# Six token tiles of an encoder block turned on VectorE in 32 by 32 blocks and by way of DRAM instead of on TensorE, with a fixed order of the second product's tiles and one convolution sum moved ahead

## The chip, the cores and the metric

The kernel runs on one core of one Trainium2 chip. The core has five engines that run their own instruction streams and wait for each other by semaphores: TensorE (PE in the profile; PEld is its weight load), VectorE (DVE), ScalarE (ACT), GpSimd (POOL) and SyncE (SP), which here issues nearly all transfers (DMAs). The metric is the device time of one launch in microseconds. Three runs of the kernel before took 1248.94, 1249.9 and 1251.17 us; their median is 1249.9 us.

## The reference

One layer of a hybrid encoder over two groups of tokens, 1024 "prompt" tokens and 256 "sample" tokens, 1024 features each, all in float32:

```python
def trunk(x, ...):
    h = rms_norm(x, norms[i, 0])
    mix = short_conv_mixer(h, conv_w_in, conv_w, conv_w_out)
    x = x + rms_norm(mix, norms[i, 1])
    h = rms_norm(x, norms[i, 2])
    return x + rms_norm(swiglu(h, ffn_w_in, ffn_w_out), norms[i, 3])

def short_conv_mixer(x, w_in, conv_w, w_out):
    b, c, v = jnp.split(x @ w_in, 3, axis=-1)      # w_in: 1024 x 3072
    u = c * v                                       # conv of width 3 over the tokens
    conv = sum(up[:, j:j + S] * conv_w[j] for j in range(3))
    return (b * conv) @ w_out                       # w_out: 1024 x 1024

def swiglu(x, w_in, w_out):                         # w_in: 1024 x 5632, w_out: 2816 x 1024
    gate, up = jnp.split(x @ w_in, 2, axis=-1)
    return (jax.nn.silu(gate) * up) @ w_out
```

With one layer (DEPTH = 1) the mLSTM mixer of the reference is never reached.

## The kernel before

Every product is done as three matmuls on float32 values split into a high and a low part (`split`: ScalarE rounds the high part, VectorE subtracts it; `TERMS` lists the three pairs). The large products are also done in Strassen-Winograd fashion, 7 products of half blocks in place of 8, so sums of blocks (`sums`, S1 to S4) are made for weights and activations by VectorE.

The kernel has four stages. **First product** (w1 and the convolution): channels lie on the partitions. Its first blocks are written out by hand in `start`; the others go through `Block` and are put in order by a scheduler that uses its own estimates. The results b * conv are stored to DRAM (`zd`) in split form. **Second product** (w2): here tokens lie on the partitions. There are ten tiles of 128 tokens, in the order ORDER2 = 0, 4, 1, 5, 2, 6, 3, 7, 8, 9; tiles 8 and 9 are the sample tokens. For each tile `load_z` brings its 1 MB of `zd` into `zs`, `mm2` does 48 matmuls of 128x512 into two PSUM banks `mx`, and then follow `norm_squares` (ScalarE, squares of `mx` summed into `j_n`), `norm_factor` (VectorE and GpSimd on single columns, `n_3t` and the like, numbered by tile), `norm_residual` (two reads of `mx` by VectorE, then the addition of `x`, whose result `x1` is stored to DRAM by SyncE), `norm_squares2` (ScalarE), `norm_factor2` and `norm_end` (VectorE; its result is `ht`). **Third product** (w3, gate and up) needs `ht` with features on the partitions, so `transposes` turns each `ht`: eight 128x128 transposes on TensorE into two PSUM banks (`tr`), which ScalarE and VectorE copy into the block buffers `ar` (a11, a12, a21, a22). `early_sums` makes parts and sums of these blocks for 128 columns at a time, and `make` prepares the first weight unit F0 (`wrf`) as `g`, `u`, `sums`, `t24`, `t13`. `entry` is the passage between the two products, written out by hand: products of tiles 8 and 9, the turning of the last tiles, the remaining sums, and the first blocks of the third product (`xf`, `yf`, `zf`). **Fourth product** (w4) follows, its order planned by the kernel's own table of costs.

In `start` the first two blocks of the w1 product are interleaved by hand; one of their additions is `ev3.add22`, which adds the bank `zb` to a copy (`c__749` in the profile); the bank is written again by a later product.

The tiles of the second product stand in a loop outside any hand-written order, so the scheduler orders them; inside `with tc.manual_schedule()` (`start`, `entry`) the instructions stand on each engine as the program text has them. Memory is handed out in places: 23 of kind "b", three of kind "a", two of kind "s"; a place that is freed goes to the end of its list, and whoever takes it waits for the last use of it. PSUM has eight banks, taken in turn. SyncE issues its transfers in order; one that waits holds up those behind it.

Of the kernel before, what the change touches and what calls it, by code (L numbers as in the profile page):

```python
# [8 lines left out]
F32 = mybir.dt.float32  # L9
F32R = mybir.dt.float32r  # L10
# [4 lines left out]
P = 128  # L15
# [21 lines left out]
def encoder_kernel(ctx: ExitStack, tc: tile.TileContext, xT, x, g0T, gB, cwT, w1, w2, w3, w4, out_p, out_s):  # L37
# [45 lines left out]


    zd = dram.tile([2, len(UNITS), P, 2, KD, P], F32, tag="zd", name="zd")
    x1d = dram.tile([NT, P, D], F32, tag="x1d", name="x1d")
    actd = dram.tile([len(UNITS), KP, P, 14 * P], F32, tag="actd", name="actd")

# [97 lines left out]
    def make(u, what):  # L186

        if u is None:
            return
        rw = raw[u]  # L190
        if what == "sums":
            sub(rw[:, 0], rw[:, 1], rw[:, 0])
            sub(rw[:, 1], rw[:, 2], rw[:, 1])
            sub(rw[:, 2], rw[:, 0], rw[:, 2])
            add(rw[:, 3], rw[:, 3], rw[:, 2])
            return
        blocks = {"g": slice(0, 4, 3), "u": slice(1, 3), "t13": slice(0, 2), "t24": slice(2, 4)}[what]
        t = wb[what, u] = get(f"w{what}{uname(u)}_", [2, 2, 512], F32R)
        split(t[:, 0], t[:, 1], rw[:, blocks])
        sums_made[u] = sums_made.get(u, 0) + what.startswith("t")  # L200
        if sums_made[u] == 2:
            put(raw.pop(u))
# [353 lines left out]
    def start():  # L556
# [209 lines left out]
        ev3.times(0, 0, ev3.t["11"])  # L766
        ev3.copy22(b3.bank["x"])
        ev.end()
        make(un, "u")
        b3.sample(evac=False)  # L770
        b3.run("x", "t24", 1, "a22", False)
# [1 line left out]
        ev3.samp_of(0, b3.bank["sg"])  # L773
        ev3.read21(b3.bank["x"])
        make(un, "sums")
        ev3.add22(b3.bank["z"])
        make(un, "t24")
        b3.run("z", "u", 1, "s4", False)
        b3.release_u()
# [26 lines left out]
    def load_z(i, k0=0, k1=KD):  # L806
        if i not in zs:
            zs[i] = get(f"zs{i}", [2, KD, P], F32R)
        src = zd[i // 4, i % 4] if i < 8 else zd[i - 8, 4]
        nc.sync.dma_start(f32(zs[i][:, :, k0:k1]), src[:, :, k0:k1])  # L810
# [35 lines left out]
    def transposes(i, banks=(None, None)):  # L846
# [17 lines left out]
                left.append((i, q, ov))  # L864
        put(hts.pop(i))

    left = []

    def take_left():
# [6 lines left out]
    def mm2(*tiles, ks=range(KD)):  # L876
        for i in tiles:
            if i not in mx:
                mx[i] = [new_ps(f"mx{i}_{h}", MX_BANKS.get((i, h))) for h in range(2)]
        for k in ks:  # L880
            for i in tiles:
                for j, (w, part) in enumerate(TERMS):
                    for h in range(2):
                        nc.tensor.matmul(  # L884
                            mx[i][h], zs[i][:, part, k], w2t[k][:, w, h * H : (h + 1) * H],
                            start=k == 0 and j == 0, stop=k == KD - 1 and j == 2,
                        )
# [35 lines left out]
        )  # L923
        put(x1)

    def after_mm2(i):
        for step in (norm_squares, norm_factor, norm_residual, norm_squares2, norm_factor2, norm_end):
            step(i)

    xts = {}  # L930

    def load_xt(i):
        xts[i] = get(f"xt{i}", [D], kind="a")
        nc.sync.dma_start(xts[i], x[i])


    a11, a12, a21, a22 = ar[0, 0], ar[1, 0], ar[0, 1], ar[1, 1]

    def early_sums(t):

        a, b, d = (q[:, :, t] for q in (a11, a21, a22))
        split(*(q[:, :, t] for q in cb["a11"]), a)
        add(b, b, d)
        sub(a, a, b)
        add(s3[:, :, t], d, a)

    F0, F1, F2 = (("f", f) for f in range(3))
    for i in ORDER2[:2]:
        load_z(i, KD - 2, KD)
    for i in ORDER2[:2]:  # L950
        load_xt(i)
    for n, i in enumerate(ORDER2[:8]):
        if n == 0:
            mm2(i, ORDER2[1])
        elif n > 1:
            early = KD - 2 if n < 4 else 4
            mm2(i, ks=range(early))
            transposes(ORDER2[n - 2])
            mm2(i, ks=range(early, KD))
            if n == 4:  # L960
                cb["a11"] = [get(f"a11{p}", [KH, 512], F32R) for p in "hl"]
                s3 = get("s3", [KH, 512])
                early_sums(slice(0, P))
            if n == 6:
                early_sums(slice(P, 2 * P))
        after_mm2(i)
        if n:
            load_z(ORDER2[n + 1])
            load_xt(ORDER2[n + 1])
        if n == 4:  # L970
            load(F0)
            for what in ("g", "u", "sums"):
                make(F0, what)
        if n == 6:
            for what in ("t24", "t13"):
                make(F0, what)


    A11, S1, S2, S4, A12, S3, A22 = range(7)
# [120 lines left out]
    def entry():  # L1100

        load_z(9)
        load(F1)
        early_sums(slice(2 * P, 3 * P))
        mm2(8, ks=range(1))
        transposes(ORDER2[6], (6, 7))
        mm2(8, ks=range(1, KD))
        norm_squares(8)
        load_xt(9)
        mm2(9, ks=range(1))  # L1110
        put(w2t[0])
        transposes(ORDER2[7], (0, 1))
        norm_factor(8)
        for k in range(1, KD):
            mm2(9, ks=range(k, k + 1))
            put(w2t[k])
        early_sums(slice(3 * P, 4 * P))
        high, low = parts_of("a12", a12)
        both(high)
        both(low)  # L1120
        make(F1, "g")
        high, low = parts_of("s2", a11)
        both(high)
        both(low)
        e0, e1 = EvF(0), EvF(1)
        b0 = Block(F0, e0, banks={q: new_ps(f"{q}f0_", b) for q, b in (("x", 6), ("y", 7))})
        b1 = Block(F1, e1, F2, ("f", 3), banks={q: new_ps(f"{q}f1_", b) for q, b in (("x", 0), ("y", 1))})
        b0.run("x", "g", 0, "a11", True)
        b0.run("y", "g", 1, "a12", True)
        b1.run("x", "g", 0, "a11", True)  # L1130
        b1.run("y", "g", 1, "a12", True)
        high, low = parts_of("s1", a21)
        both(high)
        norm_squares(9)
        norm_residual(8)
        e0.read11(b0.bank["x"])
        both(low)
        put(a21)
        norm_squares2(8)
        norm_factor(9)  # L1140
        add(e0.c11, e0.c11, b0.bank["y"])
        high, low = parts_of("s3", s3)
        both(high)
        norm_factor2(8)
        norm_residual(9)
        norm_end(8)
        e1.read11(b1.bank["x"])
        norm_squares2(9)
        add(e1.c11, e1.c11, b1.bank["y"])
        both(low)  # L1150
        put(s3)
        high, low = parts_of("a22", a22)
        both(high)
        norm_factor2(9)
        e0.silu11()
        b0.run("x", "t24", 0, "s2", False)
        e0.read12(b0.bank["x"])
        e1.silu11()
        b0.bank["z"] = new_ps("zf0_", 4)
        b0.run("z", "t13", 0, "s1", True)  # L1160
        both(low)
        put(a22)
        hs[:] = [get(f"hs{b}", [KH, 2, 256], F32R) for b in (0, 1)]
        transposes(8, (5, 2))
        b0.run("x", "t13", 1, "s3", False)
        b0.drop("t13")
        add(a12, a12, a11)
        put(a11)
        norm_end(9)
        put(gb)  # L1170
        high, low = parts_of("s4", a12)
        e0.copy22(b0.bank["x"])
        both(high)
        take_left()
        both(low)
        put(a12)
        transposes(9, (3, 1))
        b0.run("x", "t24", 1, "a22", False)
        b0.drop("t24")
        take_left()  # L1180
        add(e0.c22, e0.c22, b0.bank["z"])
        e0.read21(b0.bank["x"])
        b0.run("z", "u", 1, "s4", False)
        make(F1, "u")
        make(F1, "sums")
        e0.add12(b0.bank["z"])
        make(F1, "t24")
        b0.bank.update(sg=new_ps("sgf0_", 7), su=new_ps("suf0_", 2))
        b0.half = True
        b0.sample()  # L1190
        make(F1, "t13")
        b1.bank.update({q: new_ps(f"{q}f1_", b) for q, b in (("z", 6), ("sg", 3), ("su", 5))})
        turn[0] = 7
        load(F2)
        return b1

    def ffn_in(f):
        units = [("f", g) if g < KF else None for g in (f, f + 1, f + 2)]
        if f == 0:
            with tc.manual_schedule():  # L1200
                second.append(entry())
        elif f == 1:
            b = second[0]
            for what in ("g", "u", "sums"):
                make(F2, what)
            b.p657()
            b.sample()
            b.p43()
        else:
            b = Block(units[0], EvF(f), *units[1:], final=f == KF - 1)  # L1210
            b.p12()
            b.p657()
            b.sample()
            b.p43()
        if f % 2 and f < KF - 1:
            for _ in spill(f // 2):
                pass
# [450 lines left out]
```

## Time and profile before

| what | value |
|---|---|
| median of three timed runs | 1249.9 us |
| the profiled execution's own time | 1248.29 us |
| its span (first to last instruction) | 1246.5 us |
| granted TensorE clock | 0.998 |
| second product, first matmul of `mx` to first matmul of `xf` | 313.0 to 430.2 us |

The profile's page lists busy time by engine, the chain of work that ended last, and groups of instructions. Its further answers give waits (who waited for whom), a timeline (start, duration, engine, line, operation with its tiles, and in brackets the idle time before it and what ended it), and, for a stretch of time, the transfers with the share of the 16 DMA engines' time that their packets took. Names of tiles stand as out<-in; SPq marks the issue of a transfer by SyncE.

### The profile page before, as it was taken

To read this page: it belongs to the slowest core of one execution; us is meant where nothing else is said; L and a number is where in the kernel's file an instruction comes from. 1 tells how busy PE (TensorE), PEld (TensorE's weight loads), DVE (VectorE), ACT (ScalarE), POOL (GpSimd) and SP (SyncE) were. 2 spreads that over 40 slices of the span, in tenths; PEclk is the share of its full clock that TensorE was granted. 3 is DMA by queue.
4 is the path that set the end of the run, shared out by engine and by line. 5 is a ranking of instruction groups with operands and counts; after the bars stand their busy time and mean duration, and the time that the engine had idled before them with its cause. 6 is when DMAs were issued, how large, how long until landed. Compare 5 with 4: busy or idle time off the path is not lost.

```text
span 1246.5 us, 14942 instructions
## 1 busy us (share of the span) xinstructions
PE 1231.8 (99%) x5695; PEld 1022.9 (82%) x5695; DVE 863.1 (69%) x1225; ACT 485.5 (39%) x755; POOL 25.6 (2%) x49
## 2 busy tenths in 40 slices
PE   9999999999999999999999999999999999999997
PEld 6887888888888888888888888888888888888886
DVE  6986866758376688576576675765768478869566
ACT  8643433325233554343344343444435342202011
POOL 0000000000011000000000000000000000000000
PEclk9999999999999999999999999999999999999999
DMA  8323141416844215254352452542526798856894
GB/s 306 122 81 114 38 130 57 118 51 215 308 175 165 100 51 167 86 178 127 110 186 94 151 160 89 182 129 88 194 96 208 255 316 304 281 202 222 288 324 182
DMA packets 186120, 207.31 MB, mean 166 GB/s; under 512 B 8000, under 2 KB 146368, under 8 KB 185024
## 3 DMA queue, kind: packets, MB, share of 16 engines
q1 hardware_dynamic: 185616, 205.83, 49.1%
q8 instruction: 45, 0.74, 0.2%
q10 hardware_dynamic: 432, 0.53, 0.1%
q14 instruction: 27, 0.22, 0.1%
HBM read 134.89 MB, written 71.43 MB: 166 GB/s over the span
## 4 chain that ended last, share of the span: by engine, by line
PE 95%; DVE 1%; DMA 1%; ACT 1%; issue 1%; POOL 0%; SPq 0%; POOLq 0%; DVEq 0%
PE xo L1467 12%; PE mx L884 8%; PE zo L1467 6%; PE yo L1467 3%; PE xp__1018 L213 1%; PE xp__1382 L213 1%; PE xf__3815 L213 1%; PE xf__3359 L213 1%; PE xf__7249 L213 1%; PE xf__7082 L213 1%; PE xf__6881 L213 1%; PE xf__6719 L213 1%; PE xf__6518 L213 1%; PE xf__6356 L213 1%; PE xf__6155 L213 1%; PE xf__5993 L213 1%
## 5 line engine op out<-in xcount | busy, mean ns | idle before, releaser
L884 PE MATMUL mx<-w2s,zs 128*128 128x512 f32 x480 | 111.1, 391 | 0.0
L884 PEld LDWEIGHTS mx<-w2s,zs 128*128 128x128 f32 x480 | 89.5, 188 | 18.2
L106 ACT ACTIVATE st<-act 128x640 fp32r<-128x640 f32 x77 | 56.8, 737 | 92.2 <-DMA actd<-st 55.3
L97 DVE TENSOR_TENSOR st<-act,st 128x640 fp32r<-128x640 f32 x77 | 63.2, 821 | 20.3 <-ACT st L106 19.8
L100 DVE TENSOR_TENSOR y<-y,xo 128x512 f32<-128x512 f32 x85 | 58.2, 685 | 27.4 <-PE xo L1467 27.1
L1467 PE MATMUL xo<-w4t,us 128*128 128x512 f32 x273 | 68.9, 389 | 0.0
L1467 PEld LDWEIGHTS xo<-w4t,us 128*128 128x128 f32 x273 | 51.3, 188 | 10.6
L1467 PE MATMUL xo<-w4t,ut 128*128 128x512 f32 x222 | 55.5, 389 | 0.0
L106 ACT ACTIVATE w4t<-w4r 128x1024 fp32r<-128x1024 f32 (+1 forms) x23 | 23.5, 1023 | 72.4 <-DVE w4r L97 59.4
L1467 PEld LDWEIGHTS xo<-w4t,ut 128*128 128x128 f32 x222 | 41.7, 188 | 8.7
L100 DVE TENSOR_TENSOR y<-y,zo 128x512 f32<-128x512 f32 x45 | 30.8, 685 | 17.3 <-PE zo L1467 17.0
L1467 PE MATMUL xo<-w4b,ut 128*128 128x512 f32 x165 | 41.6, 390 | 0.0
L1467 PE MATMUL zo<-w4t,ut 128*128 128x512 f32 x165 | 41.5, 389 | 0.0
L1467 PE MATMUL zo<-w4b,ut 128*128 128x512 f32 x165 | 41.5, 389 | 0.0
L1499 ACT ACTIVATE junk<-y 128x1024 f32<-128x1024 f32 (+1 forms) x12 | 11.0, 919 | 73.7 <-DVE y L100 72.4
L1467 PEld LDWEIGHTS xo<-w4b,ut 128*128 128x128 f32 x165 | 31.0, 188 | 6.6
L1467 PEld LDWEIGHTS zo<-w4t,ut 128*128 128x128 f32 x165 | 31.0, 188 | 6.5
L1467 PEld LDWEIGHTS zo<-w4b,ut 128*128 128x128 f32 x165 | 31.0, 188 | 6.4
L459 DVE SCALAR_TENSOR_TENSOR row<-u,cw,row 128x1024 f32<-128x1024 f32 (+1 forms) x32 | 27.7, 880 | 3.3 <-ACT row L457 3.0
L106 ACT ACTIVATE w4b<-w4r 128x512 fp32r<-128x512 f32 (+1 forms) x22 | 18.1, 840 | 28.2 <-DMA us<-actd 16.0
L1467 PE MATMUL yo<-w4b,us 128*128 128x512 f32 x114 | 28.9, 389 | 0.0
L97 DVE TENSOR_TENSOR w4t<-w4r,w4t 128x1024 fp32r<-128x1024 f32 (+1 forms) x23 | 26.9, 1173 | 0.8 <-ACT w4t L106 0.8
(2372 smaller groups left out, 3313.9 us busy)
## 6 DMA issues: line engine op xcount, KB each, us to landing
actd<-st SPq DMA_DIRECT2D x154, 320.0 KB, 2.6
ut<-actd SPq DMA_DIRECT2D x20, 1024.0 KB, 7.1
us<-actd SPq DMA_DIRECT2D x62, 256.0 KB, 4.8
ut<-actd SPq DMA_DIRECT2D x16, 768.0 KB, 8.1
zd<-zst SPq DMA_DIRECT2D x32, 320.0 KB, 3.3
zs<-zd SPq DMA_DIRECT2D x8, 1024.0 KB, 6.6
w4r<-w SPq DMA_DIRECT2D x11, 512.0 KB, 4.1
w4r<-w SPq DMA_DIRECT2D x22, 256.0 KB, 5.6
```

What stands on the lines that cost most here:

```text
L97: nc.vector.tensor_tensor(out=out, in0=a, in1=b, op=ALU.subtract)
L100: return nc.vector.tensor_tensor(out=out, in0=a, in1=b, op=ALU.add)
L106: nc.scalar.activation(out, a, AF.Copy)
L213: nc.tensor.matmul(out[:, :n], stat(w, k), mov(part, k), start=first and k == 0 and j == 0, stop=last and k == KH - 1 and j == 2, skip_gro ...
L459: nc.vector.scalar_tensor_tensor(out=out, in0=src, scalar=cw[:, j, dd : dd + 1], in1=out, op0=ALU.mult, op1=ALU.add)
L884: nc.tensor.matmul(mx[i][h], zs[i][:, part, k], w2t[k][:, w, h * H : (h + 1) * H], start=k == 0 and j == 0, stop=k == KD - 1 and j == 2,)
L1467: nc.tensor.matmul(acc, stat[n, c, j][:, ap], w[wp], start=starts and jn == 0 and m == 0, stop=jn == len(grp) - 1 and m == 2, skip_group_c ...
L1499: nc.scalar.activation(junk, src, AF.Square, accum_out=acc[:, col : col + 1])
```

## The change

Tiles 0 to 5 of the second product's order (the first six) are no longer turned on TensorE. VectorE turns each `ht` in blocks of 32 by 32 (`turn_blocks`, result `vt`, in a place of kind "a"); four DMAs write `vt` to a new DRAM buffer `hd` in pieces of 32 numbers (`turn_out`); two DMAs bring it back as blocks of `ar` (`turn_in`). The seventh and the eighth tile (3 and 7) are still turned by TensorE, in `entry`. The loop over the first eight tiles becomes a function `tiles`, which now stands within the hand-written order, so all its steps follow one another on every engine as written. Two weight loads that stood early (F0) move into the fourth step, the `zs` loads run two tiles ahead, and the third part of `early_sums` moves from `entry` to the eighth step. In `start`, `ev3.add22` moves before the weight parts of the next unit.

```diff
+    hd = dram.tile([6, P, KD, P], F32, tag="hd", name="hd")
...
         ev.end()
+        ev3.add22(b3.bank["z"])
         make(un, "u")
...
         make(un, "sums")
-        ev3.add22(b3.bank["z"])
         make(un, "t24")
...
+    def turn_blocks(i):
+        h = hts.pop(i)
+        v = turned[i] = get(f"vt{i}", [4, KD, 32], kind="a")
+        nc.vector.transpose(v.rearrange("p q k t -> p k q t"), h.rearrange("p (k j q) -> p k q j", j=32, q=4))
+        put(h)
+
+    def turn_out(n):
+        v = turned.pop(ORDER2[n])
+        dst = hd[n].rearrange("(j q) k t -> j (q k) t", q=4)
+        for g in range(4):
+            nc.sync.dma_start(
+                dst[:, :, 32 * g : 32 * g + 32], v[32 * g : 32 * g + 32].rearrange("j q k t -> j (q k) t")
+            )
+        put(v)
+
+    def turn_in(n):
+        i = ORDER2[n]
+        for q in range(2):
+            nc.sync.dma_start(ar[q, i // 4][:, :, i % 4 * P : i % 4 * P + P], hd[n, :, 4 * q : 4 * q + 4])
...
-    for n, i in enumerate(ORDER2[:8]):
-        if n == 0:
-            mm2(i, ORDER2[1])
-        elif n > 1:
-            early = KD - 2 if n < 4 else 4
-            mm2(i, ks=range(early))
-            transposes(ORDER2[n - 2])
-            mm2(i, ks=range(early, KD))
...
+    def tiles():
...
+        load_z(ORDER2[2])
+        mm2(*ORDER2[:2])
+        for n, i in enumerate(ORDER2[:8]):
+            if n > 1:
+                mm2(i)
+            norm_squares(i)
+            if n != 1 and max(3, n + 2) < 9:
+                load_z(ORDER2[max(3, n + 2)])
+            if 0 < n <= VIA:
+                turn_out(n - 1)
+            norm_factor(i)
+            norm_residual(i)
+            if n:
+                load_xt(ORDER2[n + 1])
+            norm_squares2(i)
+            if 0 < n <= VIA:
+                turn_in(n - 1)
+            if n == 3:
+                load(F0)
             if n == 4:
...
+                new_parts("a11")
                 early_sums(slice(0, P))
+            if n == 5:
+                make(F0, "g")
+                make(F0, "u")
             if n == 6:
                 early_sums(slice(P, 2 * P))
...
+            if n == 7:
+                early_sums(slice(2 * P, 3 * P))
+            norm_factor2(i)
+            if n == 7:
+                make(F0, "t24")
+            norm_end(i)
+            if n < VIA:
+                turn_blocks(i)
+            if n == 6:
+                make(F0, "sums")
+            if n == 7:
+                make(F0, "t13")
...
             with tc.manual_schedule():
+                tiles()
                 second.append(entry())
```

Three places where the order on an engine moves are shown. The first is VectorE at tile 3, the seventh of the order. Before, the block copy of tile 3's neighbour and its sums stand behind `ht`:

```order
L141 SCALAR_TENSOR_TENSOR n_3t<-n_3_3061,rq 128x1
L122 TENSOR_SCALAR n_3t<-n_3t 128x1
L905 SCALAR_TENSOR_TENSOR x_3_3071<-mx_0_2994,n_3t,gb 128x512
L905 SCALAR_TENSOR_TENSOR x_3_3071<-mx_1_2995,n_3t,gb 128x512
L100 TENSOR_TENSOR x_3_3071<-x_3_3071,xt_2992 128x1024
L100 TENSOR_TENSOR n_3t<-n_3_3076 128x1
L122 TENSOR_SCALAR n_3t<-n_3t 128x1
L921 SCALAR_TENSOR_TENSOR ht_3085<-x_3_3071,n_3t,gb 128x1024
L858 COPY ar_2442<-tr_1_3129 128x4x128
```

Of the change, the same tile: the part `a11l` and the three sums (`ar`, `ar`, `s`) stand ahead of the second factor and of `ht`, and F0's weight sums (`wrf`) between `ht` and the next tile's first factor.

```order
L929 SCALAR_TENSOR_TENSOR x_3_3055<-mx_1_2990,n_3t,gb 128x512
L101 TENSOR_TENSOR x_3_3055<-x_3_3055,xt_2966 128x1024
L95 TENSOR_TENSOR a11l<-ar_2440,a11h 128x4x128
L101 TENSOR_TENSOR ar_2441<-ar_2441,ar_2443 128x4x128
L98 TENSOR_TENSOR ar_2440<-ar_2440,ar_2441 128x4x128
L101 TENSOR_TENSOR s_2881<-ar_2443,ar_2440 128x4x128
L101 TENSOR_TENSOR n_3t<-n_3_3062 128x1
L123 TENSOR_SCALAR n_3t<-n_3t 128x1
L945 SCALAR_TENSOR_TENSOR ht_3078<-x_3_3055,n_3t,gb 128x1024
L98 TENSOR_TENSOR wrf__2788<-wrf__2788 128x512 x3
L101 TENSOR_TENSOR wrf__2788<-wrf__2788 128x512
L142 SCALAR_TENSOR_TENSOR n_7t<-n_7_3134,rq 128x1
```

The second place is SyncE at the load of tile 9 (`zs_3185` before, `zs_3173` in the change). Before, it stands ahead of the store of tile 3's `x1`:

```order
L910 DMA x1d<-x_6_2974 128x1024
L934 DMA xt_3089<-x 128x1024
L810 DMA zs_3185<-zd 128x2048
L910 DMA x1d<-x_3_3071 128x1024
L934 DMA xt_3187<-x 128x1024
```

Of the change, it stands behind the store of tile 7's `x1`, two tiles later, and the stores of the turned blocks (`hd<-vt`) and their loads (`ar<-hd`) stand among the others:

```order
L881 DMA hd<-vt_2987 1024x1x32 x4
L934 DMA x1d<-x_3_3055 128x1024
L954 DMA xt_3060<-x 128x1024
L889 DMA ar_2441<-hd 128x4x128
L889 DMA ar_2443<-hd 128x4x128
L934 DMA x1d<-x_7_3144 128x1024
L954 DMA xt_3149<-x 128x1024
L811 DMA zs_3173<-zd 128x2048
```

The third place is VectorE in `start`. Before, the addition of the bank `zb` (`c__749`) stands behind the weight sums (`wrp__581`) of the next unit:

```order
L94 TENSOR_TENSOR wup__757<-wrp__581,wup__757 128x1024
L100 TENSOR_TENSOR sp__804<-sp__804,sgb__713 128x256
L103 TENSOR_TENSOR row_155<-row_155,sp__804 128x2x128
L103 TENSOR_TENSOR row_155<-row_155,xb__621 128x512
L94 TENSOR_TENSOR zst_809<-row_155,zst_809 128x640
...
L100 TENSOR_TENSOR wrp__581<-wrp__581 128x512
L100 TENSOR_TENSOR c__749<-c__749,zb__712 128x512
L94 TENSOR_TENSOR wt24p__824<-wrp__581,wt24p__824 128x1024
```

Of the change, it stands ahead of all of these:

```order
L101 TENSOR_TENSOR c__750<-c__750,zb__713 128x512
L95 TENSOR_TENSOR wup__759<-wrp__582,wup__759 128x1024
L101 TENSOR_TENSOR sp__806<-sp__806,sgb__714 128x256
L104 TENSOR_TENSOR row_156<-row_156,sp__806 128x2x128
L104 TENSOR_TENSOR row_156<-row_156,xb__622 128x512
L95 TENSOR_TENSOR zst_811<-row_156,zst_811 128x640
```

More of the change, by code (lines that the diff above doesn't have):

```diff
@@ L865, in transposes @@
         put(hts.pop(i))
+    turned = {}
+    def turn_blocks(i):
[15 more added lines that the diff above has]
+            nc.sync.dma_start(ar[q, i // 4][:, :, i % 4 * P : i % 4 * P + P], hd[n, :, 4 * q : 4 * q + 4])
     left = []
@@ L924, in norm_end @@
         put(x1)
-    def after_mm2(i):
-        for step in (norm_squares, norm_factor, norm_residual, norm_squares2, norm_factor2, norm_end):
-            step(i)
     xts = {}
@@ L937, in encoder_kernel, with new_parts @@
     a11, a12, a21, a22 = ar[0, 0], ar[1, 0], ar[0, 1], ar[1, 1]
+    def new_parts(name):
+        cb[name] = [get(f"{name}{p}", [KH, 512], F32R) for p in "hl"]
+    s3 = None
     def early_sums(t):
+        nonlocal s3
+        if s3 is None:
+            s3 = get("s3", [KH, 512])
         a, b, d = (q[:, :, t] for q in (a11, a21, a22))
@@ L947, in encoder_kernel @@
     F0, F1, F2 = (("f", f) for f in range(3))
[L948 to L951, printed above, removed]
-    for n, i in enumerate(ORDER2[:8]):
-        if n == 0:
-            mm2(i, ORDER2[1])
-        elif n > 1:
-            early = KD - 2 if n < 4 else 4
-            mm2(i, ks=range(early))
-            transposes(ORDER2[n - 2])
-            mm2(i, ks=range(early, KD))
+    VIA = 6
+    def tiles():
+        for i in ORDER2[:2]:
+            load_z(i, KD - 2, KD)
+        for i in ORDER2[:2]:
+            load_xt(i)
+        load_z(ORDER2[2])
[17 more added lines that the diff above has]
+                load(F0)
             if n == 4:
-                cb["a11"] = [get(f"a11{p}", [KH, 512], F32R) for p in "hl"]
-                s3 = get("s3", [KH, 512])
+                new_parts("a11")
                 early_sums(slice(0, P))
+            if n == 5:
+                make(F0, "g")
+                make(F0, "u")
             if n == 6:
                 early_sums(slice(P, 2 * P))
[L966 to L976, printed above, removed]
+            if n == 7:
[10 more added lines that the diff above has]
+                make(F0, "t13")
     A11, S1, S2, S4, A12, S3, A22 = range(7)
@@ L1103, in entry @@
         load(F1)
-        early_sums(slice(2 * P, 3 * P))
         mm2(8, ks=range(1))
-        transposes(ORDER2[6], (6, 7))
+        transposes(ORDER2[6], (0, 1))
         mm2(8, ks=range(1, KD))
@@ L1111, in entry @@
         put(w2t[0])
-        transposes(ORDER2[7], (0, 1))
+        transposes(ORDER2[7], (6, 7))
         norm_factor(8)
```

## The prediction

> **What bounds the kernel now.** I read the page's busy times and chain first, then TensorE's waits, then the chain and the timeline of the second product, since both edits act on waits of TensorE or on work that it loses. Busy times by engine, and the chain by engine:
>
> ```profile
> PE 1231.8 (99%) x5695; PEld 1022.9 (82%) x5695; DVE 863.1 (69%) x1225; ACT 485.5 (39%) x755; POOL 25.6 (2%) x49
> ...
> PE 95%; DVE 1%; DMA 1%; ACT 1%; issue 1%; POOL 0%; SPq 0%; POOLq 0%; DVEq 0%
> ```
>
> TensorE is the bound. Only two things can help: fewer instructions on it, or one of its few waits. The waits that concern us, in us (total, times, longest):
>
> ```profile
> PE zb__712 L213 <- DVE c__749 L100: 2.1, 1, 2.1
> PE tr L850 <- DVE n_4t L141: 1.0, 1, 1.0
> PE xp__1018 L213 <- ACT wgp__896 L93: 0.3, 1, 0.3
> ```
>
> The chain in the second product (start, us, what) is all TensorE after the first tiles:
>
> ```profile
> 313.15 20.19 PE mx L884 x89
> ...
> 344.04 1.07 PE tr L850 x8
> 345.10 10.90 PE mx L884 x48
> 356.01 0.87 PE tr L850 x8
> 356.88 8.20 PE mx L884 x36
> ...
> 420.78 9.55 PE mx L884 x42
> 430.33 2.72 PE xf__3357 L213 x12
> ```
>
> A tile's 48 matmuls take 10.9 us (0.227 each), its turning 0.9. From the first `mx` matmul (313.0; all clocks below count from it) to the first `xf` matmul is 117.3 us: 480 x 0.227 = 109.0, eight turnings 7.2, one wait of 1.0.
>
> **The change part by part: TensorE's gain.** Six turnings go: 1.1 + 5 x 0.87 = 5.4 us, and the wait of 1.0 with the first of them, -6.4 us together. With no new wait, 117.3 becomes 110.9.
>
> **VectorE in a fixed order.** This is where I expect the gain to go. Before, the scheduler put other work into VectorE's gaps; now each tile's steps run through before the next tile's begin, gaps included. One tile, on VectorE before (the first tile's factor, then tile 3):
>
> ```profile
> 334.65 0.22 DVE L141 SCALAR_TENSOR_TENSOR n_0t<-n,rq 128x1 f32<-128x1 f32 x1 [16.89 <-ACT j_n L132]
> ...
> 396.08 0.22 DVE L141 SCALAR_TENSOR_TENSOR n_3t<-n,rq 128x1 f32<-128x1 f32 x1 [2.41 <-ACT j_n L132]
> ...
> 401.48 0.16 DVE L100 TENSOR_TENSOR n_3t<-n 128x1 f32<-128x1 f32 x1 [1.40 <-ACT j_n L132]
> ...
> 402.49 1.28 DVE L921 SCALAR_TENSOR_TENSOR ht<-x,n_3t,gb 128x1024 f32<-128x1024 f32 x1 [0.66 <-POOL n_3t L123]
> 403.69 0.68 DVE L858 COPY ar<-tr 128x512 f32<-128x512 f32 x1
> 404.48 0.69 DVE L100 TENSOR_TENSOR ar<-ar,ar 128x512 f32<-128x512 f32 x1
> ```
>
> From factor to free engine: 403.69 - 396.08 = 7.6 us. No block turn is in the trace. It runs over 128x1024 numbers; its nearest row is `ht` of the same size, 1.28 us. Bounds: 0.7 (the 128x512 copy that it replaces) and 2.6 (two passes of a 1.28 row); I take 1.2, because one pass reads one input and writes one output. A tile's step is then 8.8 us, under TensorE's 10.9. [...]
>
> Extras fall into three steps. A part with three sums takes ScalarE's 0.63 and 4 x 0.69 (the last row above) = 3.4 us, in the fifth, seventh and eighth steps; F0's gate and up parts in the sixth take a ScalarE row and two VectorE rows, 1.06 + 2 x 1.23 = 3.5; F0's sums, behind `ht` in the seventh, 4 x 0.7 = 2.8:
>
> ```profile
> 391.26 0.63 ACT L93 ACTIVATE a11h<-ar 128x512 fp32r<-128x512 f32 x1
> ...
> 338.68 1.06 ACT L93 ACTIVATE wgf__2892<-wrf__2889 128x1024 fp32r<-128x1024 f32 x1 [4.06 <-DMA wrf__2889<-w]
> ...
> 339.78 1.23 DVE L94 TENSOR_TENSOR wgf__2892<-wrf__2889,wgf__2892 128x1024 fp32r<-128x1024 f32 x1 [1.11 <-ACT wgf__2892 L93]
> ```
>
> Now the calendar. The first factor comes at 334.65 - 313.0 = 21.7. The first two tiles end together on TensorE, so VectorE starts a whole step behind and never idles for TensorE. Four steps of 8.8: the fifth tile's factor at 56.9. Then 12.2 and 12.3: the seventh's at 81.4. Its `ht` is ready 7.6 + 3.4 later, at 92.4. TensorE has by then done 8 x 48 + 6 matmuls, 390 x 0.227 = 88.6, and wants to turn that tile: **a new wait of 3.8 us**. Queued behind it are the other 42 matmuls of tile 8.
>
> **SyncE and the load of tile 9.** Behind `ht` come F0's sums, so the eighth tile's factor starts at 95.2. Its `x1` is stored 4.0 us after the factor (400.11 - 396.08), at 99.2. The load of tile 9, issued at 395.97 before, now stands behind that store and one `xt` load (0.32 us an issue):
>
> ```profile
> 395.97 0.37 SPq L810 DMA_DIRECT2D zs<-zd  x1
> 400.11 0.32 SPq L910 DMA_DIRECT2D x1d<-x  x1
> ...
> zs<-zd SPq DMA_DIRECT2D x4, 1024.0 KB, 5.6
> ```
>
> It is issued at 99.9 and lands 5.6 us later (median of that stretch), at 105.5. TensorE, freed at 92.4, turns (0.9) and multiplies (42 x 0.227 = 9.5) until 102.8: **a second wait of 2.7 us**. Then 48 matmuls and the eighth tile's turning, 11.8: the first `xf` matmul at 117.3. The second product's -6.4 and +6.5 cancel.
>
> **The conv sum.** The wait of 2.1 us goes, but VectorE is full there, and its queue feeds what TensorE waits for next (VectorE; then ScalarE, SyncE, chain):
>
> ```profile
> 86.08 1.22 DVE L94 TENSOR_TENSOR wup__757<-wrp__581,wup__757 128x1024 fp32r<-128x1024 f32 x1
> ...
> 94.52 0.68 DVE L100 TENSOR_TENSOR c__749<-c__749,zb__712 128x512 f32<-128x512 f32 x1
> ...
> 99.76 1.37 ACT L93 ACTIVATE zst<-row 128x640 fp32r<-128x640 f32 x2 [3.79 <-DVE row L103]
> ...
> 88.95 14.34 SPq L469 DMA_DIRECT2D zd<-zst  x8
> 103.38 0.76 SPq L182 DMA_DIRECT2D wrp__859<-w  x1
> ...
> 103.38 5.01 DMA wrp__859<-w
> 108.42 1.07 ACT wgp__896 L93
> ```
>
> The addition now goes in at 86.08 and pushes everything up to its old place by 0.6 us. The weight sums end 0.6 later, so does the high part that ScalarE makes of them, and so do the stores `zst`. The next weights `wrp__859` are issued behind those stores, at 104.0 instead of 103.38, and `xp__1018`, which already waited for them (0.3), starts 0.6 later. So I price this edit at +0.6 us; bounds: -2.4 (both waits returned) and +0.8 (the row of 0.68 with its gap).
>
> **The transfers.** Each tile now writes 4096 pieces of 128 bytes and reads 1024 of 512. No 128-byte packet is in the trace. A stretch with stores of 512-byte packets alone, and the stretch 340 to 420 with packets of 4 KB on average:
>
> ```profile
> DMA packets 1312, 0.66 MB, mean 160 GB/s; under 512 B 32, under 2 KB 1312, under 8 KB 1312
> q1 hardware_dynamic: 1312, 0.66, 51.8%
> ...
> q1 hardware_dynamic: 3246, 13.43, 47.2%
> ```
>
> The first: 0.518 x 16 engines x 4.1 us / 1312 = 26 ns a packet. The second: 0.472 x 16 x 80 / 3246 = 186 ns for 4.1 KB. A line through both gives 9 ns for 128 bytes, the lower bound; the upper is 26, no cheaper than a 512-byte packet. On 16 engines a tile's stores cost 2.4 to 6.7 us. Per step of 10.9 us the engines also carry 2.1 MB (37.8 us / 13.43 MB x 2.1 = 5.9) and the read-back (64 x 26 ns = 1.7): 10.0 to 14.3 us. I take 14 ns, since the line is drawn far from 128 bytes: 3.6, together 11.2, 0.3 late a step, **1.5 us** over five steps; bounds 0 and 5 x 3.4 = 17. It would show as waits of TensorE for `zs`, since each load stands behind the previous tile's read-back.
>
> **Sum.** -6.4 + 3.8 + 2.7 + 0.6 + 1.5 = +2.2 us on 1248.3, the profiled execution's time; that lies 1.6 under the median of the runs. On the median: 1249.9 + 2.2 = **1252.1 us**.
>
> **Rivals.** (1) The forecast: VectorE's fixed order gives back what TensorE saves. Its own range goes from 1250 (no late transfers, a little less waiting) to 1255 (a block turn of 1.6 us: 7 x 0.4 more). Chance 0.56.
>
> (2) Faster: VectorE keeps up. The seventh tile's `ht` must be ready at 88.6 instead of 92.4, and tile 9's load issued by about 95. For it: the step of 8.8 is 2.1 under TensorE's, and half a microsecond less in each of seven steps is enough. Against it: every term of the step is a row. It decides if the step falls below 8.3. Price: -6.4 + 0.6 - up to 1.0 for the conv sum, about 1244; with half of the second wait left, 1245. Chance 0.16.
>
> (3) Slower: transfers become the bound. From 14 ns upward the engines need more than a step; at 20 ns a tile's stores take 5.1, a step 12.7, 1.8 late x 5 = 9: 1249.9 + 0.7 + 9 = about 1260; at 26 ns, 1268. For it: many small pieces, and `xt` loads, which take the freed place of `vt`, hold SyncE until the stores land. Against it: bytes are few. Chance 0.25.
>
> [...] Only its own rows could show it; nothing in the trace speaks for it, so its chance is 0.03. [...]
>
> That the conv edit does what its wait suggests (-2.1) lies within (1) and (2).
>
> **How the numbers follow.** A difference under 0.2%, 2.5 us, can't be told from none here. Case (1) has two thirds of its chance under that bound on the slower side: 0.36 same, 0.20 slower. Case (2): 0.12 faster, 0.04 same. Case (3): 0.02 same, 0.23 slower; case (4): 0.03 slower. So faster 0.12, same 0.42, slower 0.46. The range 1247 to 1264 leaves out most of (2), the upper quarter of (3) and (4), 2 in 10.
>
> **What would show it.** Right: a wait of TensorE of 3 to 5 us on `tr` for `ht` of tile 3, and one of 2 to 4 us before tile 9's `mx`, ended by a DMA of `zs`; VectorE's steps of about 8.8 us; `zb` no longer waiting, but `xp__865` or `xp__1018` waiting instead; block turns near 1.2 us. Wrong: no wait at the seventh tile's turning (then rival 2), or waits for `zs` from the third tile on and landings of `hd` above 8 us (then rival 3).

## The result and the profile after

| | before | after |
|---|---|---|
| median of the timed runs | 1249.42 us | 1263.12 us |
| the profiled execution's own time | 1248.29 us | 1263.17 us |
| second product, first `mx` to first `xf` matmul | 117.2 us | 131.9 us |

The ratio is 1.0116 (95% interval 1.0106 to 1.0127): by the ratio the change costs 14.5 us (13 to 16); the two medians lie 13.7 us apart. Nearly all of it lies in the second product: its first matmul comes 0.5 us later than before, and what follows the first `xf` takes as long as it did (816 us).

Busy times by engine, from the page of the kernel after:

```profile
PE 1232.6 (98%) x5647; PEld 1021.2 (81%) x5647; DVE 871.8 (69%) x1225; ACT 482.1 (38%) x749; POOL 26.3 (2%) x49
```

TensorE has 48 instructions fewer (the six turnings) and is busy no less. The second product as one stretch, before and after (length; busy time and instructions of each engine; granted TensorE clock, share of the DMA engines, GB/s):

```profile
313.00:430.20 117.20, 116.23 (x546) 96.68 (x545) 67.63 (x109) 40.45 (x94) 11.67 (x26) 1.00 0.54 191
```

```profile
313.50:445.30 131.80, 116.73 (x497) 94.50 (x496) 76.41 (x108) 36.38 (x87) 12.26 (x26) 0.96 0.72 216
```

Two things are in the difference. TensorE idles for 15 us of it, and it ran slower behind two of its waits. Behind the wait that ends at 430.7:

```profile
430.70:433.70 3.00, 2.98 (x8) 2.30 (x9) 2.02 (x3) 0.00 (x0) 0.00 (x0) 0.50 0.09 16
433.70:437.00 3.30, 3.30 (x14) 2.91 (x13) 1.58 (x5) 2.47 (x4) 0.53 (x1) 0.57 0.94 342
```

That is 3.0 x 0.50 + 3.3 x 0.43 = 2.9 us lost; behind the wait that ends at 388.2 it is 1.7 (a clock of 0.59 for 3.0 us, then 0.83 for 2.8), together 4.6. What TensorE idled for, in the waits of the kernel after (us in total, times, longest):

```profile
PE mx L908 <- DMA zs<-zd: 12.4, 4, 3.8
...
PE tr L851 <- DVE ht L945: 2.0, 1, 2.0
...
PE mx L908 <- DVE ar L101: 0.6, 1, 0.6
```

So the sum for the second product and what lies ahead of it is -6.4 (turnings and first wait, as forecast) + 12.4 + 2.0 + 0.6 + 4.6 + 0.5 = 13.7 us, against 14.9 between the two profiled executions. About 1 us of the rest lies in the six breaks themselves: the last matmul before each takes 0.39 us to its end, where the next would have followed after 0.23. The large term is the wait for `zs`. Where it comes from stands in SyncE's timeline, here from one load of `zs` to the next but one:

```profile
351.92 0.50 SPq L811 DMA_DIRECT2D zs<-zd  x1
354.78 5.21 SPq L881 DMA_DIRECT2D hd<-vt  x4
360.10 0.63 SPq L934 DMA_DIRECT2D x1d<-x  x1
363.86 0.34 SPq L954 DMA_DIRECT2D xt<-x  x1
364.25 0.97 SPq L889 DMA_DIRECT2D ar<-hd  x2
365.27 0.50 SPq L811 DMA_DIRECT2D zs<-zd  x1
365.82 7.88 SPq L881 DMA_DIRECT2D hd<-vt  x4
373.80 0.63 SPq L934 DMA_DIRECT2D x1d<-x  x1
376.32 0.34 SPq L954 DMA_DIRECT2D xt<-x  x1
...
379.01 0.43 SPq L811 DMA_DIRECT2D zs<-zd  x1
```

Three holds follow one another. The four stores of `vt` take 5.2 and 7.9 us to *issue* here (the first four, with nothing ahead of them, took 2.8); in the first of the two rounds SyncE has before that stood from 352.4 to 354.8, until the block turn was done. Then SyncE stands from 360.7 to 363.9 and from 374.4 to 376.3, because `xt` takes the place of `vt` and has to wait until the stores have landed. Then comes the read-back, which needs the same. Only behind it is the next `zs` issued: one every 13.5 us here, where TensorE needs one every 10.9. VectorE is in the same chain; it waits for `x1d` and `xt` in its turn:

```profile
372.66 2.01 DVE L874 STREAM_TRANSPOSE vt<-ht 128x1024 f32<-128x1024 f32 x1
...
377.48 1.41 DVE L929 SCALAR_TENSOR_TENSOR x<-mx,n_2t,gb 128x512 f32<-128x512 f32 x2 [2.52 <-DMA x1d<-x]
380.19 1.23 DVE L101 TENSOR_TENSOR x<-x,xt 128x1024 f32<-128x1024 f32 x1 [1.30 <-DMA xt<-x]
```

The block turn takes 2.0 us, not the 1.2 of the forecast.

### The profile page after: what moved, and what is told of

It is laid out like the page before. It is cut to its first block, busy times and chain, and to the rows that moved or that the text cites. A ratio compares the mean times of both kernels' runs of the same rounds, so it can differ in the third digit from the quotient of the medians.

```text
span 1261.4 us, 14894 instructions
## 1 busy us (share of the span) xinstructions
PE 1232.6 (98%) x5647; PEld 1021.2 (81%) x5647; DVE 871.8 (69%) x1225; ACT 482.1 (38%) x749; POOL 26.3 (2%) x49
## 4 chain that ended last, share of the span: by engine, by line
PE 62%; DVE 0%; issue 0%; POOLq 0%; DVEq 0%
PE xo L1513 12%; PE zo L1513 6%; PE yo L1513 3%; PE xf__6858 L214 1%; PE xf__6696 L214 1%; PE xf__6495 L214 1%; PE xf__6333 L214 1%; PE xf__6132 L214 1%; PE xf__5970 L214 1%; PE xf__5769 L214 1%; PE xf__5607 L214 1%; PE xf__5406 L214 1%; PE xf__5244 L214 1%; PE xf__5043 L214 1%; PE xf__4881 L214 1%; PE xf__4680 L214 1%
## 5 line engine op out<-in xcount | busy, mean ns | idle before, releaser
L908 PE MATMUL mx<-w2s,zs 128*128 128x512 f32 x480 | 114.8, 400 | 13.0 <-DMA zs<-zd 12.4
L101 DVE TENSOR_TENSOR y<-y,zo 128x512 f32<-128x512 f32 x45 | 30.9, 686 | 17.3 <-PE zo L1513 16.9
L133 ACT ACTIVATE j_n<-x 128x512 f32<-128x512 f32 x20 | 12.4, 624 | 64.8 <-DVE x L101 64.8
```

The costliest lines, as they stand in the source:

```text
L101: return nc.vector.tensor_tensor(out=out, in0=a, in1=b, op=ALU.add)
L133: nc.scalar.activation(junk, src, AF.Square, accum_out=acc[:, h : h + 1])
L908: nc.tensor.matmul(mx[i][h], zs[i][:, part, k], w2t[k][:, w, h * H : (h + 1) * H], start=k == 0 and j == 0, stop=k == KD - 1 and j == 2,)
```

## The experiments

Three theories were set against each other. **A**: SyncE's queue paces the tiles (holds at issue, waits for landing). **B**: VectorE does, by its fixed order and the 2.0 us turn. **C**: the DMA engines' time for the small pieces does. All ratios are against runs of the kernel before on the same chip.

### The conv sum alone

```diff
         ev.end()
+        ev3.add22(b3.bank["z"])
         make(un, "u")
...
-        ev3.add22(b3.bank["z"])
```

> The kernel before with nothing but the conv sum moved ahead (the addition of the bank zb to c__749 before the weight parts u). My theory: the wait for zb (2.1 us) goes, but the addition delays what VectorE, ScalarE and SyncE hand on, so a wait of nearly the same length stands at xp__1018 instead; in the changed kernel the first mx came 0.5 us later than before, so I expect +0.5 us (0 to +0.8). Rival: the wait of 2.1 us is returned in full, -2.1 us.

Measured: ratio 0.9999 (0.9988 to 1.0010), no difference. Its waits:

```profile
PE xp__1018 L213 <- ACT wgp__896 L93: 2.3, 1, 2.3
...
PE xp__865 L213 <- DVE wt24p__824 L94: 0.5, 1, 0.5
PE xp__865 L213 <- ACT row L106: 0.3, 1, 0.3
```

The wait for `zb` is gone, and 2.3 + 0.5 + 0.3 stand where 2.1 + 0.3 stood. The load that `xp__1018` needs in the end is issued at the same moment as before (SyncE's timeline, then TensorE's):

```profile
103.28 0.76 SPq L182 DMA_DIRECT2D wrp__859<-w  x1
...
110.60 0.50 PE L213 MATMUL xp__1018<-a11h,wgp__896 128*128 128x512 f32 x1 [2.26 <-ACT wgp__896 L93]
```

The issue is at 103.28 against 103.38, and `xp__1018` starts at 110.60 in place of 109.53. Before, ScalarE starts at 108.42, 1.1 us ahead of `xp__1018`, on the half that it needs first, which landed 5.0 us after its issue. By the same distance ScalarE starts at about 109.5 here, 6.2 us after the issue (an estimate). The changed kernel shows the same: issue at 103.30, ScalarE at 109.31, 6.0 us later, and this product at 110.42. TensorE arrives earlier at a load that comes later. Why it lands later was not looked for.

### The fixed order alone

The changed kernel without a tile by way of DRAM:

```diff
-    VIA = 6
+    VIA = 0
...
             if n > 1:
-                mm2(i)
+                mm2(i, ks=range(4))
+                transposes(ORDER2[n - 2])
+                mm2(i, ks=range(4, KD))
```

> The changed kernel with its fixed order (and the moved conv sum), but every tile turned on TensorE as before, the turning of tile n-2 amid the matmuls of tile n; no block turns, no stores of vt, no read-back. Theory A (SyncE's queue: stores of vt behind a 1 MB load hold SyncE for 7 to 9 us, and two transfers behind them wait until they have landed): no waits for zs are left, VectorE's steps are 7.6 + 0.7 us, and the extras of 3.4, 3.5, 2.8 us come too late by little; +0.5 for the conv sum and 1 to 5 us for the order, about 1253 us. Theory B (VectorE's fixed order is what costs): most of the 13.7 us stay, 1258 us or more. Theory C (the DMA engines' time for small packets): 1250 us or less, no new wait at all.

Measured: 1257.57 us, ratio 1.0053 (1.0034 to 1.0073), +6.7 us. That is nearer to B than to A's 1253, and more than C allows: without any turn on VectorE or any small piece, about half of the loss is there. Its waits in the second product and that stretch:

```profile
PE mx L908 <- DMA zs<-zd: 4.1, 1, 4.1
...
PE tr L851 <- DVE n_4t L142: 2.2, 1, 2.2
```

```profile
314.20:440.20 126.00, 119.62 (x545) 98.92 (x544) 68.07 (x108) 39.94 (x93) 12.22 (x26) 0.97 0.50 178
```

The 4.1 is tile 9's load, issued behind the eighth tile's `x1` store, as forecast; the 2.2 is the first tile's turning, which waited 1.0 before; and the lower clock behind the two waits costs about 1.7 us each (0.70 for 3.2 us, then 0.76 for 3.0, behind the 2.2; 0.50 and then 0.65, for 2.0 us each, behind the 4.1). The 2.2 is not the fixed order's: this kernel turns the first tile behind 24 matmuls of the third, the kernel before behind 36, and `ht` is ready no later (29.4 us after the first `mx` matmul, against 30.9). By these numbers some 3 us of this experiment's loss come from where it puts the turning, and the order alone costs less than 6.7. To see whether SyncE's place of the one load is the cause, it was moved:

```diff
-            if n != 1 and max(3, n + 2) < 9:
+            if n != 1 and max(3, n + 2) < 10:
...
-        load_z(9)
```

> order_alone (fixed order, all tiles turned on TensorE), but the load of zs for tile 9 is issued behind the squares of the eighth tile, ahead of that tile's x1 store, instead of behind it. If SyncE's place of that one load is what the fixed order costs (wait of 4.1 us, and 2 us of half clock behind it): 1252 us, 2 us above before. If VectorE's fixed order costs it: ht of tile 7 is late next (it was ready at 426.3 us, TensorE would want it at about 424), a wait of 2 us for ht in place of the 4.1 for zs, 1254 to 1256 us.

Measured: 1257.92 us, ratio 1.0068 (1.0051 to 1.0084), no gain, and above both expected times. The wait changes its name, as B said (the first tile's 2.2 is still there):

```profile
PE tr L851 <- DVE ht L945: 2.4, 1, 2.4
```

TensorE's second product is 1.7 us shorter in the profiled execution (124.3 for 126.0), which does not show in the time. Why VectorE is late is seen in its timeline, first of this last kernel in the fourth step, then of the kernel before in the fifth:

```profile
366.04 0.22 DVE L142 SCALAR_TENSOR_TENSOR n_5t<-n,rq 128x1 f32<-128x1 f32 x1 [3.44 <-ACT j_n L133]
...
371.50 0.16 DVE L101 TENSOR_TENSOR n_5t<-n 128x1 f32<-128x1 f32 x1 [1.47 <-ACT j_n L133]
```

```profile
375.79 1.21 DVE L94 TENSOR_TENSOR wt24f__3091<-wrf__2889,wt24f__3091 128x1024 fp32r<-128x1024 f32 x1
376.92 1.22 DVE L100 TENSOR_TENSOR x<-x,xt 128x1024 f32<-128x1024 f32 x1
378.06 0.68 DVE L858 COPY ar<-tr 128x512 f32<-128x512 f32 x1
...
380.02 0.69 DVE L100 TENSOR_TENSOR ar<-ar,ar 128x512 f32<-128x512 f32 x1
```

In the fixed order VectorE idles 3.4 and 1.5 us in a step that has no extra work, and the extra work comes in a lump in the steps behind. The scheduler had put a weight part, a block copy and a sum between the pieces of one tile.

### Small pieces and landings, two by two

One kernel stores `vt` in runs of 4 KB instead of pieces of 128 bytes; one lets nothing on SyncE wait for stores that were just issued; one does both.

```diff
             nc.sync.dma_start(
-                dst[:, :, 32 * g : 32 * g + 32], v[32 * g : 32 * g + 32].rearrange("j q k t -> j (q k) t")
+                hd[n, 32 * g : 32 * g + 32].rearrange("p k t -> p (k t)"),
+                v[32 * g : 32 * g + 32].rearrange("j q k t -> j (q k t)"),
             )
```

> The changed kernel, but each of the four stores of vt writes 32 runs of 4 KB instead of 1024 pieces of 128 bytes: the same bytes from the same places in another layout, so the blocks of ar hold the features and tokens in a wrong order (the arithmetic that follows is the same). The block turn, the order and the number of DMAs stay. Theory A (SyncE held by the stores): SyncE's issue of four stores falls from 7 to 9 us to below 2.5, zs issues come 10 to 11 us apart instead of 13.4, TensorE's waits for zs fall from 12.4 us to under 3; what is left is VectorE's step with a block turn of 2.0 us (step 9.6, seventh tile late by 5 to 8 us): 1254 to 1257 us. Theory B (VectorE's fixed order and turn): no change from the changed kernel beyond 3 us, 1260 us or more. Theory C (packet time on the DMA engines): as A.

```diff
-                turn_out(n - 1)
+            if 1 < n <= VIA + 1:
+                turn_in(n - 2)
+            v = turn_out(n - 1) if 0 < n <= VIA else None
...
                 load_xt(ORDER2[n + 1])
+            if v is not None:
+                put(v)
```

> The changed kernel with its small pieces, but nothing on SyncE between two loads of zs waits until the stores of vt have landed: xt takes the place that the residual addition has just freed instead of vt's, and the read-back of a tile is issued one step later, behind the next load of zs. Theory A (SyncE's queue: waits for landing and the hold of the stores add up to 13.4 us a cycle): the 3.5 to 4.5 us of the two waits go, zs issues come 10 to 11 us apart, TensorE's waits for zs fall under 5 us, VectorE's waits for x1d and xt go too; the seventh tile's turning waits 5 to 8 us for VectorE: 1255 to 1258 us. Theory C (the DMA engines' time for 4096 small packets a tile): the same packets cross in the same time, waits for zs stay above 9 us, 1260 us or more. Theory B (VectorE's order and turn): 1258 to 1262 us, waits for ht in place of waits for zs.

> pieces_4k and no_landing together: stores in runs of 4 KB (features and tokens in a wrong order) and no wait on SyncE for their landing. If SyncE's holds and the packets' time were all that delays zs, no wait for zs is left but tile 9's (2 us); VectorE is then the bound alone: the wait for ht of tile 3 grows from 4.0 and 5.3 to 6 to 7.5 us, since less is lost ahead of it, and the time is that of pieces_4k, 1254 to 1256 us. If VectorE were not the bound: 1250 to 1252 us.

| | zs issues apart | wait for `zs` | wait for `ht` | time | ratio to before |
|---|---|---|---|---|---|
| changed kernel | 13.4 us | 12.4 us | 2.0 us | 1263.12 us | 1.0116 (1.0106 to 1.0127) |
| no wait for landing | 12.1 | 5.5 | 5.3 | 1257.9 | 1.0059 (1.0039 to 1.0078) |
| runs of 4 KB | 11.4 | 5.5 | 4.0 | 1256.05 | 1.0047 (1.0032 to 1.0061) |
| both | 10.5 | 1.3 | 6.8 | 1255.7 | 1.0051 (1.0036 to 1.0066) |

(The distance is the mean over four, from the load of the fifth tile of the order to that of the ninth.) The waits of the three kernels, in the order of the table:

```profile
PE mx L908 <- DMA zs<-zd: 5.5, 3, 3.0
PE tr L851 <- DVE ht L945: 5.3, 1, 5.3
```

```profile
PE mx L908 <- DMA zs<-zd: 5.5, 4, 2.2
PE tr L851 <- DVE ht L945: 4.0, 1, 4.0
```

```profile
PE tr L851 <- DVE ht L945: 6.8, 1, 6.8
...
PE mx L908 <- DMA zs<-zd: 1.3, 2, 1.1
```

Either edit alone takes 7 of the 12 us of waits for `zs`, both together nearly all: A holds, though each edit alone left more than A foresaw (under 5 us without waits for landing, under 3 with 4 KB runs). The 4 KB runs do not tell A from C, since they shorten SyncE's hold and the DMA engines' time together; the edit without waits for landing is A's alone. With 4 KB runs the issue of four stores falls to 1.7 to 2.4 us:

```profile
354.67 1.86 SPq L880 DMA_DIRECT2D hd<-vt  x4
```

C holds in part. Without waits for landing the loads are still 12.1 us apart, and the DMA engines are busy 89% of the stretch 345 to 420; whether the stores' hold on SyncE (4.9 to 9.0 us there) or the DMA engines' time keeps them apart was not separated. But the time of all four stays about 6 us or more above before, since what is taken from the wait for `zs` comes back in the wait for `ht`: B is the second bound, right behind the first.

### The block turn

> The changed kernel with six forms of the turn, one for each tile in the order 0, 4, 1, 5, 2, 6: as it is; with dense input (neighbouring numbers of a row form a block); with dense output only; dense on both sides; a plain copy of the same 128x1024 numbers instead of a turn; two turns of half the size. Except for the first and the last tile the features come out in a wrong order, the work after it is the same. A look at VectorE's duration alone. As it is 2.0 us. If the strided reading (every fourth number) costs the 0.8 us over my estimate of 1.2, dense input and dense on both sides take 1.2 us. If the turn itself costs it, all turns take 2.0 us and only the copy 1.2 (the 128x512 copy takes 0.68). The two halves: 2 x 1.0 if the time goes by size, more if there is a start-up of the turn.

Six forms in one kernel, in the order named (line 878 is the copy):

```profile
343.34 1.99 DVE L889 STREAM_TRANSPOSE vt<-ht 128x1024 f32<-128x1024 f32 x1
353.13 1.25 DVE L887 STREAM_TRANSPOSE vt<-ht 128x1024 f32<-128x1024 f32 x1
362.05 2.02 DVE L885 STREAM_TRANSPOSE vt<-ht 128x1024 f32<-128x1024 f32 x1
373.40 1.25 DVE L883 STREAM_TRANSPOSE vt<-ht 128x1024 f32<-128x1024 f32 x1
389.17 0.69 DVE L878 COPY vt<-ht 128x1024 f32<-128x1024 f32 x1
404.17 1.09 DVE L880 STREAM_TRANSPOSE vt<-ht 128x512 f32<-128x512 f32 x1
```

Reading every fourth number is what costs 0.75 us: with 32 neighbours the turn takes 1.25, whatever the order in which it writes. The second half-size turn took 1.04, the two halves 2.13 against 1.99 for the whole, so the time goes by size here. Is it what made the kernel slow?

```diff
-        nc.vector.transpose(v.rearrange("p q k t -> p k q t"), h.rearrange("p (k j q) -> p k q j", j=32, q=4))
+        nc.vector.transpose(v.rearrange("p q k t -> p k q t"), h.rearrange("p (k q j) -> p k q j", j=32, q=4))
```

> The changed kernel with a block turn that reads 32 neighbouring numbers instead of every fourth one (features come out in a wrong order). The turn falls from 2.0 to 1.25 us, the 1.2 of my prediction, six times. If SyncE's chain of stores and landings paces the tiles, VectorE only waits longer for xt and x1d: less than 2 us gained, 1260.5 to 1263 us. If VectorE's step paces them: 4 to 5 us, 1258 to 1259 us.

Measured: 1263.66 us, ratio 1.0114 (1.0101 to 1.0128), the changed kernel's time. All six turns take 1.25 us (7.5 in total), and TensorE waits for `zs` nearly as long (for `ht` 1.1 in place of 2.0); its second product takes 131.8 us as in the changed kernel:

```profile
L874 DVE STREAM_TRANSPOSE vt<-ht 128x1024 f32<-128x1024 f32 x6 | 7.5, 1245 | 0.2
```

```profile
PE mx L908 <- DMA zs<-zd: 11.7, 6, 4.0
```

4.5 us less on VectorE bring nothing while SyncE paces the tiles.

### Towards a better version

The first try, on the kernel without waits for landing, moved the turn into the gap in which VectorE waits for ScalarE's squares, one step later:

```diff
             norm_squares2(i)
+            if 0 < n <= VIA:
+                turn_blocks(ORDER2[n - 1])
+                put(turn_out(n - 1))
```

> no_landing with three more edits: VectorE turns a tile not behind its own ht, but one step later, in the gap in which it waits for ScalarE's squares of x1 (1.5 us idle a step); the stores of vt are issued there; tile 9's zs is loaded ahead of the eighth tile's x1 store. VectorE's step falls from 9.6 to about 8.2 us. If VectorE's step is what is left of the loss in no_landing (wait of 5.3 us for ht of tile 3): that wait falls under 1 us, 1251 to 1253 us. If the DMA engines' time (89% busy in no_landing) is: waits for zs of 4 to 6 us before tiles 2, 6 and 3 stay or grow, 1255 to 1258 us.

Measured: 1260.0 us, ratio 1.0088 (1.0073 to 1.0103), worse than either case foresaw. The edit also moved who takes which place: `x1` now got that of `vt`, and VectorE itself waited for the stores to land, 3.7 to 6.0 us a step:

```profile
368.36 1.41 DVE L929 SCALAR_TENSOR_TENSOR x<-mx,n_5t,gb 128x512 f32<-128x512 f32 x2 [5.97 <-DMA hd<-vt]
```

It says nothing on VectorE's step; a landing has to be kept off every queue, VectorE's included. The next version gives `vt` back behind `norm_end`, sends only every second tile through DRAM, and fills VectorE's gaps by hand (`gapfill(k)` does the next k of a list of block sums, sums of F0 and weight parts):

```diff
+    VIA = (0, 2, 4)
...
             norm_factor(i)
+            gapfill(1)
             norm_residual(i)
...
             norm_squares2(i)
+            v = None
+            if n - 1 in VIA:
+                turn_blocks(ORDER2[n - 1])
+                v = turn_out(n - 1)
+            else:
+                gapfill(2)
+            norm_factor2(i)
+            gapfill(1)
+            norm_end(i)
+            if v is not None:
+                put(v)
```

> A version in which the causes found so far are taken away. Only tiles 0, 1 and 2 (the first, third and fifth of the order) go by way of DRAM, so that a step with stores is followed by one without; VectorE turns a tile one step later, in the gap in which it waits for ScalarE's squares of x1; nothing on SyncE waits for stores that were just issued; tile 9's zs is loaded ahead of the eighth tile's x1 store; the sums of the blocks and of F0 are taken apart and put one by one into VectorE's gaps; ScalarE makes both block copies of the tiles that TensorE turns; the conv sum stands where it was before. TensorE loses three turnings (2.6 us) and the first tile's wait of 1.0. If the waits that those edits remove are all that made the changed kernel slow: no wait of TensorE over 1 us from the first mx to the first xf, that stretch 114 us instead of 117.2, 2 to 3 us under before (1246.5 to 1248). If transfers, or VectorE's time as such, are still the bound: waits for zs or ht of 2 us and more, 1250 to 1254 us.

> The version called three with no tile by way of DRAM: all tiles turned on TensorE, everything else in the same order. It tells whether a gain of that version comes from the turning or from its order. If the turning on VectorE is worth what TensorE no longer does: 3 turnings (2.6 us) more and the wait for the first tile's ht back (2.2 us, and about 1.6 of half clock behind it, as in order_alone), 1251 to 1253 us. If the order alone makes the gain: the same time as that version, within 1 us.

Measured: 1250.07 us, ratio 1.0000 (0.9990 to 1.0011), for three tiles by way of DRAM; 1251.9 us, ratio 1.0020 (1.0011 to 1.0029), for none. The difference is not the turning alone: the latter turns its first tile behind 24 matmuls too and waits 2.2 us for it. One wait is left in the former, and a lower clock behind it (first the wait, then the three stretches that follow it):

```profile
PE mx L908 <- DMA zs<-zd: 2.5, 1, 2.5
```

```profile
361.60:364.00 2.40, 2.40 (x7) 1.92 (x8) 1.41 (x2) 0.00 (x0) 0.00 (x0) 0.67 1.12 377
364.00:366.00 2.00, 2.00 (x6) 1.54 (x5) 1.80 (x2) 0.51 (x1) 0.00 (x0) 0.55 0.95 368
366.00:369.00 3.00, 3.00 (x14) 2.44 (x13) 2.31 (x4) 0.83 (x4) 0.55 (x1) 1.00 0.87 307
```

That load of `zs` stood behind the first tile's stores. They were moved behind it:

```diff
                 load_z(ORDER2[max(3, n + 2)])
+            if n == 2:
+                v0 = turn_out(0)
```

> The version called three with one move: the four stores of the first tile's vt are issued one step later, behind the load of zs for the fifth tile of the order instead of ahead of it (its read-back one step later too). In that version this load was issued at 353.9 us, right behind those stores (3.8 us of issue), landed at 361.6, and TensorE waited 2.5 us for it and ran its next 72 matmuls 1.6 us slower than others. If that wait is what is left of the loss: no wait for zs, 3 to 4 us less, 1245.5 to 1247.5 us, faster than before by 0.2 to 0.3%. If the move only puts the wait elsewhere (the same bytes in the same time): a wait for zs of 2 us or more at that tile or the next, 1249 to 1251 us.

Measured: 1246.9 us, ratio 0.9985 (0.9975 to 0.9995): 1.9 us faster than before (0.6 to 3.1). This version beats both kernels, the one before by 0.15%. Its second product:

```profile
312.50:426.90 114.40, 113.57 (x521) 94.16 (x520) 68.95 (x103) 40.12 (x94) 13.73 (x26) 1.00 0.71 223
```

It is 114.4 us long: 117.2 less three turnings (2.6) and the first wait (1.0), plus the one wait for `zs` that is left (0.8). So in this stretch a turning taken from TensorE is worth what the prediction said, once nothing has to wait for it.

## Why the prediction was right and wrong

The range, 1247 to 1264 us, held the time, and "slower" was the likeliest sign. The likeliest case, 1252.1 us, was 11 us off. That the range held was luck for the most part: the time lies in its upper end, which stood for rival (3), whose price was wrong. Step by step:

- **TensorE's gain of 6.4 us** was right; the last version confirms its terms.
- **VectorE's step of 8.8 us** was 9.7, from the factor of the third tile to that of the fourth, where VectorE waited for no DMA. It is 7.6 + 2.0: the block turn was mis-sized, 2.0 for 1.2, within its bounds of 0.7 and 2.6. The nearest row, `ht` by its size, has no strided reading of the turn's kind. In the time of the changed kernel the error is worth nothing, as the dense turn showed.
- **The wait for `ht` of tile 3**, 3.8 us, was 2.0, because the waits for `zs` ahead of it had made TensorE late itself. With those taken away it is 6.8: the calendar with a turn of 2.0 gives 3.8 + 6 x 0.8 = 8.6, and TensorE had waited 0.9 us itself ahead of it.
- **The second wait, for tile 9's `zs`**, 2.7 us, was 3.6, by the mechanism named. The fixed order alone has it without any store (4.1), and moving that load shows what the step left out: `ht` of tile 7 is late instead.
- **The conv sum**, +0.6, was right within what can be told, and `xp__1018` does start later, by 0.9 us in the changed kernel. The mechanism was another: `wrp__859` is issued when it was, not later, but lands later (6.0 us after its issue in the changed kernel, 5.0 before).
- **The transfers, +1.5 us, are the step that failed.** Its price of 14 ns a packet was good. The transfers of the changed kernel and of the one with 4 KB runs from 345 to 420 us (packets, MB, share of the DMA engines; and KB each, median us to landing):

```profile
q1 hardware_dynamic: 33444, 18.53, 88.1%
...
hd<-vt SPq DMA_DIRECT2D x24, 128.0 KB, 6.6
```

```profile
q1 hardware_dynamic: 10523, 19.51, 76.3%
```

  These are 1057 and 916 us of engine time. In the second, 768 packets of 4 KB carry `vt`, 143 us at the prediction's 186 ns; the other 773 us moved 16.4 MB, which makes 727 for the 15.4 MB that are no `vt` in the first. By this estimate 24,576 pieces of 128 bytes took 330 us, 13 ns each. The 66 us a DMA engine was busy are 11.0 to 11.8 a tile (6 tiles' stores in the stretch, or 5.6 tiles at 13.4 us), where I had 11.2. What failed is the sentence "0.3 late a step": it lets the engines run without a break, so that only their time over 10.9 counts. SyncE issues in order, and I gave its issues no time beyond 0.32 us and its waits none at all. The stores' hold, the wait of `xt` for `vt`'s place and that of the read-back left the engines 12% idle in a stretch in which they had no time to spare. I had seen the place of `vt`, and named it for rival (3), without pricing it.
- **Rival (3)** foretold the time, 1260 to 1268, and the sign that would show it, waits for `zs`. Its price did not hold: packets did not take 20 to 26 ns, `hd` landed in 6.6 us, not above 8, and the first late tile was the fifth. Of its mechanism the clause that `xt` holds SyncE until the stores land was the true part.
- **Rival (4)**, a far slower kernel at a chance of 0.03, did not come. No run shows a 128-byte piece that costs more than the 26 ns of a 512-byte packet in the trace before: by the estimate above it took 13.
- **Rival (2)** needed VectorE's step below 8.3; it was 9.7.
- **Left out altogether** were the 4.6 us of lower clock behind TensorE's waits.

## What to carry to other kernels

Work that was taken from the busiest engine paid here only once that engine hardly waited behind the replacement (13.7 us lost with 15.0 us of waits, 1.9 gained with 0.8): before pricing transfers by bytes or packets, write down the issuing queue's own loop (time to issue, what place each transfer takes, whose landing it waits for) and compare its length with the step. A hand-written order replaces a scheduler's gap filling too, and has to do that work itself. After one bound is taken away, price the next before believing the gain: here a tile took TensorE 10.9 us, the DMA engines 11 to 12, VectorE 9.7 and, in the steps with extra work, about 3 more, and SyncE 13.4.

## What the runs showed of the hardware

- Issuing took long in the changed kernel: four stores of 1024 pieces each held SyncE 2.8 us with an idle queue and 5.2 to 9.1 us behind a 1 MB load, where four stores in 4 KB runs held it 1.7 to 2.4 us. The four together held SyncE 6.7 us in the mean, about as long as one of them took to land (6.6 us, the median), and half of its 13.4 us a tile.
- Some waits of TensorE cost more than their length here. Behind waits of 2.2, 2.5, 3.6 and 3.8 us the granted clock was 0.50 to 0.83 for the next 4 to 6 us, 1.7 to 2.9 us lost each; behind others of 2.4 to 2.65 us (changed kernel, and the one with the turn in the gap) it stayed at 1.00. A wait of 2.2 us was thus followed by a drop and one of 2.65 was not; what sets the two kinds apart was not shown.
- The block turn of 128x1024 float32 numbers took 1.25 us with a dense read, 2.0 with a read of every fourth number, and a plain copy 0.69.
